# A first load of two rows a partition in place of one, and one load instead of two ahead of the entry barrier

## The chip, the cores and the metric

The kernel runs on one core of one Trainium2 chip. The metric is the device time of one execution in microseconds. The time before is 161.78 us, the median of 9 runs that lie between 161.64 and 162.16 us. Five kinds of engine matter here: VectorE (DVE in the profile) and ScalarE (ACT) compute, GpSimd (POOL) does small finishing work, SyncE (SP) issues every load and store, and the DMA engines move the data.

## The reference

The input `x` has 32 x 512 rows of 1024 float32 numbers, 16,384 rows or 67.1 MB. The result is one number a row:

```
relu_x = np.maximum(x, 0)
return np.mean(relu_x, axis=-1).astype(np.float32)
```

So every byte of 67.1 MB has to be read once from device memory, and 64 KB are written.

## The kernel before

The 16,384 rows lie one after another in memory, 4 KB each. The first 128 of them form a block of their own: partition p gets row p, into the tile `row0`. The other 16,256 rows are split so that each of the 128 partitions owns 127 consecutive rows (`J`), so the rows of neighbouring partitions start 127 rows, or 508 KiB, apart.

A partition's 127 rows are loaded in order, by SP, through one DMA queue: seven big loads of 16 rows a partition (`NB` = 16, 8 MB each, numbered t = 0 to 6) into three buffers in turn (`BUFS` = 3), then pieces of 7, 4, 2 and 1 rows (`row_pieces`), and then the last row in column pieces of 512, 256 and 256 (`col_pieces`). Each load has a semaphore of its own in `loaded`. Before a buffer is used again, SP waits in `buf_free` (lines 111 to 115) until ACT and DVE have finished with its previous content.

ACT and DVE share the rows: rows with an even number go to ACT (`act_row`, line 13: one activation with Relu whose accumulator gives the sum), rows with an odd number to DVE (`dve_row`, line 18). Both wait for the load in `rows` (line 144). POOL scales the sums by 1/1024 in `finish` (line 153). At the end the last full row is split between ACT and DVE, and of the very last row ACT takes 512 columns, DVE 256 and then, on line 197, the remaining 256 with the scaling and the sum of the row in one instruction. SP then stores `res` (line 205), clears the semaphores and waits on line 210 until the stores have landed.

The block `row0` is treated apart. ACT reduces it in one activation (line 164; its activation table is loaded just ahead, after the wait for the load), DVE turns the 128 results from a column into rows (line 168), and SP stores them with a small DMA (line 125) that is issued behind the load t = 3.

The program opens with entry barriers, in which every engine drains, reports and waits for a release (line 232 of the launch code and line 55 in the profile). The function `issue_ahead_of_entry_barrier(nc, n)` takes the first n loads out of SP's body and puts them ahead of SP's first drain, so that they are issued before the barrier. Before, n is 2: the load of `row0` (512 KB) and the load t = 0 (8 MB) go out ahead of the barrier, and t = 1 and t = 2 follow after it.

Of the kernel before, what the change touches and what calls it, by code (L numbers as in the profile page):

```python
# [9 lines left out]
ACT = mybir.ActivationFunctionType  # L10
# [15 lines left out]
def issue_ahead_of_entry_barrier(nc, n):  # L26


    entry = nc.cur_f.blocks[0].instructions
    for _ in range(n):  # L30
        body, load = next(
            (block.instructions, k)
            for block in nc.cur_f.blocks[1:]
            for k, ins in enumerate(block.instructions)
            if ins.opcode == "DMACopy"
        )
        first = body[load]
        assert first.engine == mybir.EngineType.SP and not first.sync_info.on_wait
        assert all(i.opcode in ("Drain", "EventSemaphore") or i.engine != first.engine for i in body[:load])
        del body[load]  # L40
        at = next(k for k, i in enumerate(entry) if i.engine == first.engine and i.opcode == "Drain")
        entry.insert(at, first)
# [3 lines left out]
def kernel(  # L46
# [10 lines left out]
    nc = tc.nc  # L57
    P = nc.NUM_PARTITIONS
    xf = x.flatten_outer_dims()
    R, D = xf.shape  # L60
    assert R % P == 0
    J = R // P
    inv = 1.0 / D

    xfirst, xmain = xf[:P, :], xf[P:, :]
    outfirst, outmain = out.flatten()[:P], out.flatten()[P:]
    J = J - 1
    xr = xmain.rearrange("(p j) d -> p j d", p=P, j=J)
    outr = outmain.rearrange("(p j) -> p j", p=P, j=J)

    NB = 16
    BUFS = 3
    full = J // NB

    row_pieces = [7, 4, 2, 1]
    assert full * NB + sum(row_pieces) + 1 == J
    col_pieces = [512, 256, 256]
    assert sum(col_pieces) == D

    def sbuf(name, *shape):  # L80
        return ctx.enter_context(nc.sbuf_tensor(name, list(shape), F32))

    bufs = [sbuf(f"rows{b}", P, NB, D) for b in range(BUFS)]
    sums, res, part = sbuf("sums", P, J), sbuf("res", P, J), sbuf("part", P, 2)


    last = sbuf("last", P, D + 2)
    scale = sbuf("scale", P, D // 4 + 2)

    row0, mean0, turned0 = sbuf("row0", P, D), sbuf("mean0", P, 32), sbuf("turned0", P, 32)  # L90


    loaded = [nc.alloc_semaphore(f"loaded{i}") for i in range(full + len(row_pieces) + len(col_pieces) + 1)]
# [1 line left out]
    first = nc.alloc_semaphore("first")  # L95
    stored = nc.alloc_semaphore("stored")
# [11 lines left out]
    def load(i, dst, src):  # L108
        nc.sync.dma_start(out=dst, in_=src).then_inc(loaded[i], 16)

    def buf_free(t):

        if t >= BUFS:
            nc.sync.wait_ge(act, t - BUFS + 1)
            nc.sync.wait_ge(dve, t - BUFS + 1)

    for t in range(full):
        buf_free(t)
        if t == 0:
            load(-1, row0[:, :], xfirst)  # L120
        load(t, bufs[t % BUFS][:, :, :], xr[:, t * NB:(t + 1) * NB, :])
        if t == BUFS:

            nc.sync.wait_ge(first, 2)
            nc.sync.dma_start(
                out=outfirst.rearrange("(q i) -> q i", i=32), in_=turned0[0:P:32, :],
            ).then_inc(stored, 16)
    j0 = full * NB
    buf_free(full)
    xt = bufs[full % BUFS]  # L130
    lo, i = 0, full
    for n in row_pieces:
        load(i, xt[:, lo:lo + n, :], xr[:, j0 + lo:j0 + lo + n, :])
        lo, i = lo + n, i + 1
    c = 0
    for w in col_pieces:
        load(i, last[:, c:c + w], xr[:, J - 1, c:c + w])
        c, i = c + w, i + 1
# [14 lines left out]
    def finish(after, lo, hi):  # L153
# [7 lines left out]
    nc.scalar.wait_ge(pool, 1)  # L161
    nc.vector.wait_ge(pool, 1)
    nc.scalar.wait_ge(loaded[-1], 16)
    nc.scalar.activation(  # L164
        out=row0[:, :], in_=row0[:, :], func=ACT.Relu, scale=inv, accum_out=mean0[:, 0:1],
    ).then_inc(first, 1)
    nc.vector.wait_ge(first, 1)
    nc.vector.transpose(turned0[:, :], mean0[:, :]).then_inc(first, 1)  # L168
    for t in range(full):
# [2 lines left out]
    lo, i = 0, full  # L172
    for n in row_pieces[:-1]:
        rows(i, xt, lo, n, j0)
        lo, i = lo + n, i + 1
# [12 lines left out]
        out=res[:, J - 2:J - 1], in0=part[:, 0:1], scalar1=part[:, 1:2], scalar2=inv, op0=ALU.add, op1=ALU.mult,  # L188
# [9 lines left out]
        out=last[:, 768:], in0=last[:, 768:], scalar=0.0, in1=scale[:, :], op0=ALU.max, op1=ALU.mult,  # L198
        accum_out=res[:, J - 1:J],
# [7 lines left out]
    used = [s.num for s in (*loaded, act, dve, pool, first)]  # L207
    assert used == list(range(used[0], used[0] + len(used)))
    nc.sync.sem_clear(range(used[0], used[-1] + 1))
    nc.sync.wait_ge(stored, 32).then_inc(stored, -32)  # L210

    for e, hint in zip(hinted, hints):
        e.br_lt(flag, 1, on_true="rows_begin", on_false="rows_end").branch_hint(hint)
    nc.br("rows_end", engines=[e for e in mybir.ALL_ENGINES if e not in (h.engine for h in hinted)])
    nc.switch_bb("rows_end")

    issue_ahead_of_entry_barrier(nc, 2)


# [28 lines left out]
```

## Time and profile before

| what | value |
|---|---|
| median of 9 runs | 161.78 us (161.64 to 162.16) |
| the profiled execution's own time | 161.89 us |
| its span | 160.5 us |
| DVE busy | 73.3 us, 46% of the span |
| ACT busy | 70.4 us, 44% of the span |
| DMA queue of the loads, share of the span | 97.3%, 67.18 MB |
| SP issues `row0`, t = 0, t = 1, t = 2 at | 0.00, 0.45, 1.92, 2.30 us |
| ACT has `row0` at | 3.44 us |
| ACT and DVE start on t = 0, 1, 2, ..., 6 at | 23.30, 42.66, 62.01, ..., 139.41 us |
| DVE's last instruction starts | 158.44 us |
| SP issues the last store at | 158.59 us |

Times inside an execution are counted from the start of the span, which is SP's first DMA issue. SPq is the queue of SP's issues. A DMA engine's packet is one descriptor: 4 KB for a row of `row0`, 64 KB for the 16 rows of a partition in a big load; a 4-byte packet is an engine's report to the semaphore. A load has landed when all 16 engines have reported.

### The profile page before, as it was taken

The page shows a single profiled execution, that of the slowest core. Times are in us where ns is not written, and L with a number is a line of the kernel's source. Part 1 is how long each engine was busy: PE and PEld are TensorE (multiplying, and loading weights), DVE is VectorE, ACT ScalarE, POOL GpSimd, SP SyncE. Part 2 cuts the span into 40 slices and gives each one's busy share as a digit, 9 for nine tenths or more (in the row PEclk, how much of TensorE's full clock was granted, in tenths as well). Part 3 has the DMA queues.
Part 4 walks back from the last instruction along what each step waited for, and adds up shares of the span by engine and source line. Part 5 has one row for each costly group of instructions (what it writes and reads, how often), then busy time and mean ns, then how long its engine had stood idle before and what let it go on. Part 6 is the DMA issues. An engine that isn't in the chain of part 4 may idle for free. (4 is left out here: it accounts for less than half of the span.)

```text
span 160.5 us, 347 instructions
## 1 busy us (share of the span) xinstructions
DVE 73.3 (46%) x131; ACT 70.4 (44%) x133; POOL 1.3 (1%) x9
## 2 busy tenths in 40 slices
DVE  0000019900399005970079500993009920299884
ACT  1400019900397005950079300991009900299983
POOL 1000000000000000000000000000000000000001
DMA  9969979979979989999899899899699699799991
GB/s 392 490 294 523 474 310 523 474 310 523 441 343 523 425 359 523 392 392 523 376 408 523 359 425 523 359 425 523 278 506 523 261 523 506 302 407 438 408 397 39
DMA packets 2313, 67.18 MB, mean 418 GB/s; under 512 B 393, under 2 KB 649, under 8 KB 1033
## 3 DMA queue, kind: packets, MB, share of 16 engines
q1 hardware_dynamic: 2312, 67.18, 97.3%
q14 instruction: 1, 0.00, 0.0%
HBM read 67.11 MB, written 0.07 MB: 418 GB/s over the span
## 5 line engine op out<-in xcount | busy, mean ns | idle before, releaser
L20 DVE TENSOR_SCALAR_CACHE_REDUCE rows<-rows 128x1024 f32<-128x1024 f32 (+1 forms) x63 | 72.1, 1208 | 78.9 <-DMA rows<-in_x_dram 78.8
L15 ACT ACTIVATE rows<-rows 128x1024 f32<-128x1024 f32 x64 | 66.2, 1035 | 84.1 <-DMA rows<-in_x_dram 83.9
L15 ACT ACTIVATION_READ_ACCUMULATOR rows<-rows 128x1 f32 x64 | 11.9, 187 | 0.0
L20 DVE DVE_READ_ACCUMULATOR rows<-rows 128x1 f32 x63 | 5.2, 83 | 0.0
L168 DVE STREAM_TRANSPOSE turned<-mean 128x32 f32<-128x32 f32 x1 | 0.2, 213 | 6.0 <-ACT row L164 6.0
L164 ACT ACT_TABLE_LOAD x1 | 1.3, 1283 | 3.4 <-DMA row<-in_x_dram 3.4
L157 POOL TENSOR_SCALAR res<-sums 128x112 f32<-128x112 f32 (+1 forms) x2 | 0.5, 248 | 154.1 <-DVE rows L20 154.1
L164 ACT ACTIVATE row<-row 128x1024 f32<-128x1024 f32 x1 | 1.1, 1056 | 0.0
L15 ACT ACTIVATE last<-last 128x512 f32<-128x512 f32 x1 | 0.6, 630 | 0.0
L20 DVE TENSOR_SCALAR_CACHE_REDUCE last<-last 128x256 f32<-128x256 f32 x1 | 0.4, 419 | 0.2 <-DMA last<-in_x_dram 0.2
L197 DVE SCALAR_TENSOR_TENSOR last<-last,scale 128x258 f32<-128x258 f32 x1 | 0.4, 428 | 0.1
L142 POOL MEMSET scale<- 128x258 f32 x1 | 0.3, 313 | 0.0
L187 POOL TENSOR_SCALAR res<-part 128x1 f32<-128x1 f32 x1 | 0.3, 264 | 0.6 <-DVE rows L20 0.6
L164 ACT ACTIVATION_READ_ACCUMULATOR row<-row 128x1 f32 x1 | 0.2, 187 | 0.0
L15 ACT ACTIVATION_READ_ACCUMULATOR last<-last 128x1 f32 x1 | 0.2, 186 | 0.0
L141 POOL MEMSET mean<- 128x32 f32 x1 | 0.1, 124 | 1.5 <-POOLq L55 1.5
L232 POOL MEMSET const-bfloat16-1.0<- 128x1 bf16 x1 | 0.1, 101 | 0.0
L232 POOL MEMSET const-uint8-127<- 128x1 uint8 x1 | 0.1, 101 | 0.0
L232 POOL MEMSET const-float32-0.0<- 128x1 f32 x1 | 0.1, 98 | 0.2 <-issue 0.2
L232 POOL MEMSET const-float32-1.0<- 128x1 f32 x1 | 0.1, 98 | 0.0
L197 DVE DVE_READ_ACCUMULATOR last<-last,scale 128x1 f32 x1 | 0.1, 83 | 0.0
L20 DVE DVE_READ_ACCUMULATOR last<-last 128x1 f32 x1 | 0.1, 82 | 0.0
## 6 DMA issues: line engine op xcount, KB each, us to landing
rows<-in_x_dram SPq DMA_DIRECT2D x1, 3584.0 KB, 37.9
rows<-in_x_dram SPq DMA_DIRECT2D x1, 2048.0 KB, 42.4
rows<-in_x_dram SPq DMA_DIRECT2D x1, 1024.0 KB, 44.4
row<-in_x_dram SPq DMA_DIRECT2D x1, 512.0 KB, 3.4
rows<-in_x_dram SPq DMA_DIRECT2D x1, 512.0 KB, 45.2
last<-in_x_dram SPq DMA_DIRECT2D x1, 256.0 KB, 45.4
last<-in_x_dram SPq DMA_DIRECT2D x2, 128.0 KB, 45.2
rows<-in_x_dram SPq DMA_DIRECT2D x7, 48.7
```

Source lines behind the costliest of these rows:

```text
L15: return nc.scalar.activation(out=src, in_=src, func=ACT.Relu, accum_out=acc)
L20: return nc.vector.tensor_scalar(out=src, in0=src, scalar1=0.0, scalar2=init, op0=ALU.max, op1=ALU.add, accum_out=acc,)
L141: nc.gpsimd.memset(mean0[:, :], 0.0)
L142: nc.gpsimd.memset(scale[:, :], inv).then_inc(pool, 1)
L157: nc.gpsimd.tensor_scalar(out=res[:, lo:hi], in0=sums[:, lo:hi], scalar1=inv, scalar2=0.0, op0=ALU.mult, op1=ALU.add,)
L164: nc.scalar.activation(out=row0[:, :], in_=row0[:, :], func=ACT.Relu, scale=inv, accum_out=mean0[:, 0:1],).then_inc(first, 1)
L168: nc.vector.transpose(turned0[:, :], mean0[:, :]).then_inc(first, 1)
L187: nc.gpsimd.tensor_scalar(out=res[:, J - 2:J - 1], in0=part[:, 0:1], scalar1=part[:, 1:2], scalar2=inv, op0=ALU.add, op1=ALU.mult,).then_i ...
L197: nc.vector.scalar_tensor_tensor(out=last[:, 768:], in0=last[:, 768:], scalar=0.0, in1=scale[:, :], op0=ALU.max, op1=ALU.mult, accum_out=r ...
L232: nc = _bacc.Bacc("TRN2", target_bir_lowering=False, num_devices=1)
```

## The change

The first two blocks of 128 rows are now both kept apart. Partition p gets row p of each, so `row0` holds two rows a partition and is loaded by one DMA of 1 MB with 256 descriptors of 4 KB. The rest is 126 rows a partition, so neighbouring partitions now start 504 KiB apart. The piece of 7 rows becomes one of 6; the big loads and the other pieces keep their sizes. ACT reduces the two rows of `row0` in two activations and reports after the second, DVE still turns them in one instruction, and SP stores them with two small DMAs, so the last wait is for 48 instead of 32. Only the load of `row0` is issued ahead of the entry barrier; the load t = 0 comes after it, ahead of t = 1 and t = 2.

```diff
-    xfirst, xmain = xf[:P, :], xf[P:, :]
-    outfirst, outmain = out.flatten()[:P], out.flatten()[P:]
-    J = J - 1
+    xfirst, xmain = xf[:2 * P, :].rearrange("(c p) d -> p c d", c=2), xf[2 * P:, :]
+    outfirst, outmain = out.flatten()[:2 * P], out.flatten()[2 * P:]
+    J = J - 2
...
-    row_pieces = [7, 4, 2, 1]
+    row_pieces = [6, 4, 2, 1]
...
-    row0, mean0, turned0 = sbuf("row0", P, D), sbuf("mean0", P, 32), sbuf("turned0", P, 32)
+    row0, mean0, turned0 = sbuf("row0", P, 2, D), sbuf("mean0", P, 32), sbuf("turned0", P, 32)
...
-            load(-1, row0[:, :], xfirst)
+            load(-1, row0[:, :, :], xfirst)
...
-            nc.sync.dma_start(
-                out=outfirst.rearrange("(q i) -> q i", i=32), in_=turned0[0:P:32, :],
-            ).then_inc(stored, 16)
+            for c in range(2):
+                nc.sync.dma_start(
+                    out=outfirst[c * P:(c + 1) * P].rearrange("(q i) -> q i", i=32), in_=turned0[c:P:32, :],
+                ).then_inc(stored, 16)
...
-    nc.scalar.activation(
-        out=row0[:, :], in_=row0[:, :], func=ACT.Relu, scale=inv, accum_out=mean0[:, 0:1],
-    ).then_inc(first, 1)
+    for c in range(2):
+        done = nc.scalar.activation(
+            out=row0[:, c, :], in_=row0[:, c, :], func=ACT.Relu, scale=inv, accum_out=mean0[:, c:c + 1],
+        )
+    done.then_inc(first, 1)
...
-    nc.sync.wait_ge(stored, 32).then_inc(stored, -32)
+    nc.sync.wait_ge(stored, 48).then_inc(stored, -48)
...
-    issue_ahead_of_entry_barrier(nc, 2)
+    issue_ahead_of_entry_barrier(nc, 1)
```

## The prediction

> **What bounds the kernel now.** I read the page's busy shares first, then the waits, then the timeline of the start and of the end, and last the records of single DMA packets and semaphore updates in the trace.
>
> ```profile
> span 160.5 us, 347 instructions
> ...
> DVE 73.3 (46%) x131; ACT 70.4 (44%) x133; POOL 1.3 (1%) x9
> ...
> q1 hardware_dynamic: 2312, 67.18, 97.3%
> ```
>
> Neither compute engine is busy half of the span; the queue of loads fills 97.3% of all 16 DMA engines' time. The waits say the same: ACT and DVE wait for nothing but loads.
>
> ```profile
> ACT rows L15 <- DMA rows<-in_x_dram: 83.9, 9, 17.4
> DVE rows L20 <- DMA rows<-in_x_dram: 78.8, 8, 17.1
> ```
>
> So the end is: when the stream of loads starts to flow, plus its bytes at the engines' rate, plus a tail behind the last piece. The timeline shows the start and the rate. Its columns are start, duration, engine, line, operation.
>
> ```profile
> 0.00 0.39 SPq L109 DMA_DIRECT2D row<-in_x_dram  x1
> ...
> 0.45 1.80 SPq L109 DMA_DIRECT2D rows<-in_x_dram  x2
> 1.93 0.12 POOL L141 MEMSET mean<- 128x32 f32 x1 [1.49 <-POOLq L55]
> ...
> 3.44 1.28 ACT L164 ACT_TABLE_LOAD   x1 [3.44 <-DMA row<-in_x_dram]
> ...
> 23.30 1.06 ACT L15 ACTIVATE rows<-rows 128x1024 f32<-128x1024 f32 x1 [17.42 <-DMA rows<-in_x_dram]
> ...
> 42.66 1.06 ACT L15 ACTIVATE rows<-rows 128x1024 f32<-128x1024 f32 x1 [10.94 <-DMA rows<-in_x_dram]
> ```
>
> From one big load to the next is 19.36 us (42.66 - 23.30), and the later ones agree (62.01, 81.36, 100.71, 120.06, 139.41). In the packet records a 64 KB packet takes 2.420 us (median of 896); each engine has 8 a load, 8 x 2.420 = 19.36. The engines are never without a packet in the middle, so nothing there can be won or lost except through the packets' own duration.
>
> The start is different. The packets of `row0` begin at 1.02 us, take 0.159 us each and follow at 0.1555 us. The engines finish their 8 between 2.44 and 2.93 us. Fifteen of the 16 start their first 64 KB packet between 2.50 and 2.93 us, but one of the three that had finished by 2.45 starts it only at 3.58: it idles some 1.13 us. That lag is never made up, because every engine has the same bytes. The last of the 16 reports of t = 0 comes at 23.27, the one before at 22.87; for the last piece of all it is 157.86 and 157.50. So 0.36 us of the end hangs on one engine that started late.
>
> The end, in the timeline:
>
> ```profile
> 155.30 1.22 DVE L20 TENSOR_SCALAR_CACHE_REDUCE rows<-rows 128x1024 f32<-128x1024 f32 x1
> ...
> 156.59 0.58 ACT L15 ACTIVATE rows<-rows 128x448 f32<-128x448 f32 x1
> ...
> 157.26 0.63 ACT L15 ACTIVATE last<-last 128x512 f32<-128x512 f32 x1
> ...
> 157.79 0.19 ACT L15 ACTIVATION_READ_ACCUMULATOR last<-last 128x1 f32 x1
> ...
> 158.08 0.43 DVE L197 SCALAR_TENSOR_TENSOR last<-last,scale 128x258 f32<-128x258 f32 x1
> ...
> 158.59 0.35 SPq L205 DMA_DIRECT2D out_dram<-res  x1
> ```
>
> The reader is to see that each piece is taken up as it lands and that the tail simply follows the landings.
>
> **The change part by part.** The sum is made against the profiled execution, 161.89 us (span 160.54, and 1.35 around it). It lies 0.11 over the median of the runs.
>
> *The entry barrier.* The instructions of the barrier show who holds it:
>
> ```profile
> L232 POOLq EVENT_SEMAPHORE  x2: 17/17/17, 1.1 to 1.2; - x2
> ...
> L232 SPq DRAIN  x1: 125/125/125, 0.9 to 0.9; - x1
> ```
>
> POOL's collecting semaphore at 1.07 comes right behind SP's drain (0.92 to 1.05); the others had drained by 0.48. With one issue less ahead of it, SP drains 0.47 us earlier (0.92 - 0.45), and what SP issues first after the barrier moves from 1.92 to about 1.45. That is now t = 0. Its issue is thus 1.0 us later than before (0.45 to 1.45); t = 1 and t = 2 follow at about 1.83 and 2.21 and are needed only 20 and 39 us later. ACT, DVE and POOL leave the barrier earlier too, for nothing: ACT waits for `row0` anyway.
>
> *The cover of the later issue.* `row0` is now 16 packets of 4 KB an engine, 8 x 0.1555 = 1.24 us more, so the engines finish it between 3.69 and 4.17. How long after its issue t = 0 can flow is bounded by rows of the trace: the last store's first packet came 0.84 us after its issue (158.59, 159.44), `row0`'s first packets 1.02 to about 1.3, most engines had t = 0 within 2.05 (0.45 to 2.50), and the late engine 3.14 (0.45 to 3.58). So t = 0 is there at 2.3, 2.75, 3.5 or, on one engine, 4.6 us. I take the middle two, as cold issues from SP of the same kind: it waits in the queue before `row0` is done, and no engine idles. If the issue of 256 descriptors takes longer than 0.39, it costs nothing until it is 0.2 us longer by the third of these values; issues of 128 descriptors took 0.33 to 0.49 and one of 4 descriptors 0.64, so the count does not show in them.
>
> *The bytes.* They are the same. Eight packets of 4 KB an engine take the place of 32 KB in the 7-row piece: 1.244 us for 8 x (1.062 - 0.911) = 1.21 us, where 0.911 is interpolated between the 16 KB (0.611) and 28 KB (1.062) packets. Cost +0.03.
>
> *The late engine.* If it is gone, the end follows the next engine, 0.36 us earlier: -0.36. If an engine is again 1.13 late, it starts t = 0 at 4.83 instead of 3.58 with 1.21 us of work more behind it: +0.04.
>
> *The row distance.* 504 instead of 508 KiB between partitions. In the trace 64 KB packets take 2.418 at best and 2.42 nearly always, but the first of each engine took up to 2.70, and in the wave around 32 us all took 2.43. So their duration does depend on how the streams lie. Bounds: all at 2.418 (8 x 7 x 0.002 = -0.1 us) to all at 2.434 (+0.8 us). I take 0, as 15 of 16 packets in mid-stream sit at 2.42.
>
> The Trainium skill's page "DMA: Bandwidth & Descriptors", section "Latency and other measured facts", speaks against this part: it lists copies whose partitions lie large powers of two apart as slower, 207 against 214 GB/s at 512 KiB, and the change moves the distance from 4 to 8 KiB short of 512. The same entry says that 4 KiB off was enough for the full rate, and the rows here, 508 KiB apart, run at 2.42 us a packet. If 504 KiB lost what the page has for 512, an estimate by its figures is 3.4% of 155 us, 5 us more; by the packet rows it is nothing.
>
> *ACT, DVE and the small store at the start.* A second activation of 1.06 us with its 0.19 read, all at 5 to 9 us, when ACT has nothing until 23.3: cover of 14 us, cost 0. It would cost its 1.04 us if t = 0 had landed. The second store of `turned0` has four packets of 128 B, each some 0.015 us on its engine, the late one among them: +0.015. Its issue (0.64) stands in SP's queue at 33 us, ahead of the load that waits for its buffer until 51.9, so nothing waits for it.
>
> *The tail.* The 6-row piece leaves DVE less time. Count from the start on t = 6 (139.41 before). DVE's rows follow each other at 1.14 us. The 4-row piece comes at 13.40 - 1.21 = 12.19, but DVE has 11 rows by then, until 12.54: late by 0.35. The 2-row piece comes at 14.68, DVE is free at 14.82; the 1-row piece at 15.97, DVE is free at 15.96. So it has just caught up, cost 0, and behind it DVE still has the 0.22 us that it waits for its first column piece. ACT has 11 rows x 1.04 = 11.4, before 12.19. The last store writes 504 instead of 508 bytes a partition: 0.
>
> Sum: -0.36 + 0.03 + 0.015 = -0.32, so 161.57 on the profiled execution's 161.89. The median of the runs is 0.11 lower, which I read as a late engine that is mostly a little less late; without it the runs would come down to the same place. I predict 161.56, 0.14% under the median. No change is what a measurement of this kernel cannot tell from zero, 0.2% or 0.32 us, so this lies within it.
>
> **The rivals.** *The late engine is late again.* What speaks for it: I can't say from the trace why it idled; its `row0` was done and the load had been issued 2 us before. If its cause is the change-over from one load to the next, it is in the new kernel too. Against: the 9 runs spread over 0.5 us, so it varies. With a gap of 1.13 us: 161.89 + 0.04 = 161.93, no change.
>
> *Slower: a later t = 0, or streams that hinder each other longer, at the first change-over.* Place: between `row0`'s last packet and an engine's first 64 KB. It decides from the point where any engine starts t = 0 after 5.0 us (4.79 is even with 161.89, and 162.10 is 0.2% over the median). The late engine's 3.14 us after the new issue would give 4.59, so it needs 0.4 more, an issue of `row0` of 0.8 us for its 256 descriptors; or a gap of 1.3 instead of 1.13. With twice the gap, 2.26, the start is at 5.96 and the time 161.89 + 1.17 = 163.06. For it: all first packets were slowed (2.42 to 2.70), so the streams do hinder each other at this point, and the row distance changes how. Against: 15 of 16 engines did not idle.
>
> *Slower all along.* Every packet at 2.434: 161.56 + 0.8 = 162.4 or more. Only a few waves show that now.
>
> *Faster by more.* The first packets' excess (0.02 to 0.28 over 2.42, in the mean 0.13) shrinks, since the engines finish 1 MB more spread out: 161.56 - 0.2 = 161.35.
>
> **How the numbers follow.** Back to back 0.45 (161.3 to 161.75, some two fifths of it under 161.46), the late engine as before 0.25 (a fifth of it over 162.10), slower at the change-over 0.20, slower all along 0.05, faster by more 0.05. Faster: 0.18 + 0.05, and a little for a gap that shrinks without going, 0.25. Slower: 0.20 + 0.05 + 0.05 = 0.30. Same: the rest, 0.45. Range 161.25 to 162.3: it leaves out the all-along case, half of the change-over case and a small part below, 0.2 in all.
>
> **What would show it.** SP's drain at about 0.45 and t = 0 issued at 1.4 to 1.8. ACT has `row0` at 4.6 to 4.8. With no late engine ACT and DVE start on t = 0 at 24.1 to 24.2 (23.30 + 1.21 - 0.33), and 24.5 with it; every later load 19.36 on. DVE without a pause from t = 6 to the last full row. It would be wrong if the steps between the big loads leave 19.36, if `row0` lands after 5 us, or if DVE reaches the split row after ACT.

## The result, and the profile after

The changed kernel takes 162.52 us, the median of 11 runs (162.31 to 163.12); the kernel before, 161.85 us over 34 runs. The ratio is 1.0043, with a 95% interval of 1.0032 to 1.0053: slower by 0.43%, some 0.7 us. The profiled execution took 162.43 us.

The page of the changed kernel has the same picture in the large, half-idle compute engines and a full queue of loads. The start, in its timeline:

```profile
0.00 0.45 SPq L109 DMA_DIRECT2D row<-in_x_dram  x1
...
1.50 1.39 SPq L109 DMA_DIRECT2D rows<-in_x_dram  x3
...
5.48 1.28 ACT L166 ACT_TABLE_LOAD   x1 [5.48 <-DMA row<-in_x_dram]
...
25.21 1.06 ACT L15 ACTIVATE rows<-rows 128x1024 f32<-128x1024 f32 x1 [16.25 <-DMA rows<-in_x_dram]
...
44.56 1.06 ACT L15 ACTIVATE rows<-rows 128x1024 f32<-128x1024 f32 x1 [10.92 <-DMA rows<-in_x_dram]
```

The reader is to see three things. SP issues t = 0 at 1.50 us, as foreseen. `row0` reaches ACT at 5.48, not at 4.6 to 4.8. And t = 0 is taken up at 25.21, not at 24.1 to 24.2. From there the step is 19.35 us again (44.56 - 25.21). So all of the loss has arisen by the time t = 0 has landed.

The end, in the same timeline, shows DVE without a pause, and at the split row (157.30) together with ACT, as foreseen:

```profile
153.86 1.21 DVE L20 TENSOR_SCALAR_CACHE_REDUCE rows<-rows 128x1024 f32<-128x1024 f32 x1
...
155.00 1.21 DVE L20 TENSOR_SCALAR_CACHE_REDUCE rows<-rows 128x1024 f32<-128x1024 f32 x1
...
156.01 1.06 ACT L15 ACTIVATE rows<-rows 128x1024 f32<-128x1024 f32 x1 [0.30 <-DMA rows<-in_x_dram]
156.14 1.21 DVE L20 TENSOR_SCALAR_CACHE_REDUCE rows<-rows 128x1024 f32<-128x1024 f32 x1
...
157.30 0.75 DVE L20 TENSOR_SCALAR_CACHE_REDUCE rows<-rows 128x576 f32<-128x576 f32 x1
157.30 0.58 ACT L15 ACTIVATE rows<-rows 128x448 f32<-128x448 f32 x1
...
159.34 0.35 SPq L208 DMA_DIRECT2D out_dram<-res  x1
```

The sum in the profiled executions: the last report of the last piece moves from 157.86 to 158.61, +0.75; from there to the last store's issue it is 0.73 in both; the last store takes 1.74 instead of 1.95 us, -0.21. Together +0.54, which is 162.43 - 161.89. (The last store's time is not the change's: with 504 bytes a partition it took 1.80 and 2.11 in the profiles of two kernels below.)

The records of single packets say where the 0.75 us arose:

| | before | after |
|---|---|---|
| the engines finish `row0` between | 2.44 and 2.93 us | 4.25 and 5.05 us (predicted: 3.69 and 4.17) |
| time that `row0`'s packets took over 0.159 each, mean of an engine | 0.23 us | 0.75 us |
| idle between `row0` and the first 64 KB packet | 1.13 us on one engine | none over 0.04 us |
| first 64 KB packets | 2.42 to 2.70 us | 2.42 to 2.72, one 3.68 us |
| last two of the 16 reports of the last piece | 157.50, 157.86 | 158.20, 158.61 |

Fifteen engines are late because `row0` itself went slowly: its packets between 1.1 and 2.9 us took up to 0.83 us instead of 0.16. That moves the last report but one by 0.70 (157.50 to 158.20). The sixteenth had 1.26 us in the first packet of t = 0, where before one engine had idled 1.13; its lag at the end is 0.41 instead of 0.36. Together that is the 0.75. The first 64 KB packets as a whole are no slower than before: 0.12 us over 2.42 in the mean of the 16, against 0.13. No engine was out of packets, so the cover held in the sense of the prediction, and yet it cost.

### The profile page after: what moved, and what is told of

Same layout as the page of the kernel before. It is cut to its first block, busy times and chain, and to the rows that moved or that the text cites. A ratio compares the mean times of both kernels' runs of the same rounds, so it can differ in the third digit from the quotient of the medians.

```text
span 161.1 us, 348 instructions
## 1 busy us (share of the span) xinstructions
DVE 73.0 (45%) x131; ACT 70.3 (44%) x133; POOL 1.3 (1%) x9
## 5 line engine op out<-in xcount | busy, mean ns | idle before, releaser
L15 ACT ACTIVATE rows<-rows 128x1024 f32<-128x1024 f32 (+1 forms) x63 | 65.1, 1035 | 82.9 <-DMA rows<-in_x_dram 82.8
L166 ACT ACTIVATE row<-row 128x1024 f32<-128x1024 f32 x2 | 2.1, 1048 | 0.0
```

What stands on the lines that cost most here:

```text
L15: return nc.scalar.activation(out=src, in_=src, func=ACT.Relu, accum_out=acc)
L166: done = nc.scalar.activation(out=row0[:, c, :], in_=row0[:, c, :], func=ACT.Relu, scale=inv, accum_out=mean0[:, c:c + 1],)
```

## The experiments

All ratios are against the kernel before, run on the same chip beside the variant, with 95% intervals. "Stretch" is what the first 64 KB packet of each engine took over 2.42 us, as the mean of the 16, in the one profiled execution; it leaves out idle time and `row0`'s own packets, which the table at the end has beside it. Diffs are against the changed kernel unless said otherwise.

**Both loads ahead of the barrier again.**

```diff
-    issue_ahead_of_entry_barrier(nc, 1)
+    issue_ahead_of_entry_barrier(nc, 2)
```

> The changed kernel with both loads ahead of the entry barrier again: only the order of issues is undone. Theory 'pattern' (the two rows of one partition, 512 KiB apart in memory, slow the first packets of the first load: 0.55 to 0.83 us instead of 0.17 to 0.39): row0 still reaches ACT at 5.4 to 5.5 us and the time stays at 162.5, within 0.15. Theory 'issue' (the later issue of t = 0 slows the start): row0 reaches ACT at about 4.6 and the time falls to 161.9. Theory 'count' (256 descriptors of one DMA come too slowly): as 'pattern', 162.5.

Ratio 0.9993 (0.9983 to 1.0004). The whole loss is gone, with two blocks, 126 rows and the two-row load in place. Its timeline:

```profile
0.00 0.45 SPq L109 DMA_DIRECT2D row<-in_x_dram  x1
...
0.49 2.32 SPq L109 DMA_DIRECT2D rows<-in_x_dram  x3
...
4.94 1.28 ACT L166 ACT_TABLE_LOAD   x1 [4.94 <-DMA row<-in_x_dram]
...
24.20 1.06 ACT L15 ACTIVATE rows<-rows 128x1024 f32<-128x1024 f32 x1 [15.77 <-DMA rows<-in_x_dram]
```

`row0` is there at 4.94 instead of 5.48, and t = 0 is taken up 1.01 us earlier than in the changed kernel. Every first 64 KB packet takes 2.42, stretch 0.00, and no engine is late (last two reports 157.71 and 157.72). So 'issue' holds for the time; the first packets of `row0` are still slow (eight took 0.7 to 0.9 us), so that part is not the later issue's.

**The first load in other forms, t = 0 still after the barrier.** Adjacent rows, rows 516 KiB apart, and two loads of one block each:

```diff
-    xfirst, xmain = xf[:2 * P, :].rearrange("(c p) d -> p c d", c=2), xf[2 * P:, :]
+    xfirst, xmain = xf[:2 * P, :].rearrange("(p c) d -> p c d", c=2), xf[2 * P:, :]
```

> The changed kernel with rows 2p and 2p+1 in partition p, so that its 8 KB lie together; the results of the first 256 rows come out in another order. 'Pattern': row0 reaches ACT at 4.6 to 4.7 us, 161.85. 'Issue': 5.4, 162.5. 'Count': 4.6, since it is 128 descriptors again if the two rows become one, 161.85.

Ratio 1.0077 (1.0058 to 1.0096), stretch 0.52, and one engine idle for at least 0.8 us: slower still.

```diff
-    xfirst, xmain = xf[:2 * P, :].rearrange("(c p) d -> p c d", c=2), xf[2 * P:, :]
+    xfirst, xmain = xf[:2 * (P + 1), :].rearrange("(c p) d -> p c d", c=2)[:P], xf[2 * P:, :]
```

> The changed kernel with row p and row 129 + p in partition p, so that the two rows are 516 instead of 512 KiB apart; row 128 is left out and row 256 read twice. 256 descriptors of 4 KB as in the change. 'Pattern', if it is the distance of 512 KiB: row0 reaches ACT at 4.6 to 4.7 us, 161.85. 'Issue' and 'count': 5.4, 162.5.

Ratio 1.0018 (1.0005 to 1.0032); the profiled execution, at 162.81 us the slowest of its 12, has a stretch of 0.39. In between the two theories, so it settles little: the loss is smaller than in the changed kernel, and not gone.

```diff
...
-            load(-1, row0[:, :, :], xfirst)
+            for c in range(2):
+                nc.sync.dma_start(out=row0[:, c, :], in_=xfirst[:, c, :]).then_inc(loaded[-1 - c], 16)
...
-    issue_ahead_of_entry_barrier(nc, 1)
+    issue_ahead_of_entry_barrier(nc, 2)
```

> The changed kernel with the two blocks loaded by two DMAs of 128 descriptors each, both ahead of the barrier; t = 0 still after it. 'Pattern': the engines read one block after the other, row0 is complete at 4.6 to 4.7 us, 161.85. 'Issue': t = 0 is later still, 162.5 or more. 'Count': 161.85. In all of these one engine is again 1.1 to 1.3 us late into t = 0, if that is a fixed cost of the change-over from 4 KB to 64 KB packets, and its last report comes 0.4 us behind the others'.

Ratio 1.0029 (1.0016 to 1.0041), stretch 0.15, one engine 0.33 us behind the next at the end. `row0` was complete on the engines at 3.85 to 4.22, where the prediction had it: its packets went faster, and the median was slower all the same (the profiled execution, 161.84, is near the fast end of its 12, 161.69 to 162.75). 'Pattern' and 'count' fall as the cause of the whole.

**One row, only its load ahead of the barrier** (against the kernel before: `issue_ahead_of_entry_barrier(nc, 1)`).

> The kernel before with only the load of row0 ahead of the entry barrier; one row, 127 rows a partition. Theory 'late issue' (an issue of t = 0 at about 1.5 instead of 0.45 us costs by itself, whatever covers it): slower by 0.5 to 0.9 us, 162.2 to 162.6 on a before of 161.7, with row0's packets or the first 64 KB packets stretched by several tenths. Theory 'cover' (it costs only as far as row0's packets don't cover it, and one row covers less than two): the engines idle from 2.5 to 2.9 until 2.8 to 3.5 us, so it is slower too, by 0.3 to 0.6, but with gaps instead of stretched packets.

Ratio 1.0076 (1.0052 to 1.0100). Both gaps and stretch: the engines finish `row0` at 2.49 to 2.95, start t = 0 at 2.63 to 3.98, and the first packets take 2.66 to 3.16 us, stretch 0.47. So the later issue costs some 1.2 us with a cover of one row and some 0.8 with two (1.0043 against 0.9993). In these two pairs more cover helps a little, but two rows are not enough; with two adjacent rows a partition the same step costs 1.3 us (1.0077, and 0.9994 in the last pair below).

**Two loads and t = 0, all three ahead of the barrier** (the two-load kernel above with n = 3).

> Two blocks by two DMAs, and t = 0, all three ahead of the barrier; 126 rows a partition. 'Late issue': 161.6, as fast as with the two-row load and t = 0 ahead (0.9993 of before), and the first 64 KB packets at 2.42 to 2.5. If the two-row load itself was what made that one clean, the first 64 KB packets stay at 2.5 to 2.7 and the time at 161.8 or above.

Ratio 1.0044 (1.0027 to 1.0060), stretch 0.62, against the 161.6 us that 'late issue' had foreseen. Here t = 0 was issued ahead of the barrier, at 0.91 us, and the loss came back. It is not the barrier, then. Nor is it simply the time of the issue: with t = 0 at 1.93 us, 1.0 us later, the same two loads were no slower (1.0029).

**t = 1 and t = 2 issued late**, in the changed kernel and in the kernel before:

```diff
         buf_free(t)
+        if t == 1:
+            nc.sync.wait_ge(first, 2)
```

> The changed kernel with t = 1 and t = 2 issued only when row0 has been reduced, at about 9 us instead of 1.9 and 2.4 us; t = 1 is needed at 24 us, so the wait itself costs nothing. Theory 'later issues' (the issues of t = 1 and t = 2 fall into the start of the stream and slow it): the stretched packets at 2.0 to 2.9 and of the first 64 KB wave go, 161.7 to 162.0. Theory 'late issue': they stay, 162.3 to 162.6.

Ratio 1.0037 (1.0021 to 1.0052), stretch 0.54.

> The kernel before with t = 1 and t = 2 issued only when row0 has been reduced, at about 6.3 us. 'Later issues': the first 64 KB packets fall from 2.43 to 2.70 to 2.42 and no engine is late, 161.3 to 161.5, faster than before. 'Late issue': no change, 161.7.

Ratio 0.9996 (0.9979 to 1.0013), stretch 0.19. The loss stays in the first and does not turn into a gain in the second, so the later issues have no part in it that these runs can tell.

**A first load with the row distance of t = 0**, once with t = 0 after the barrier and once, in the kernel before, ahead of it:

```diff
-            load(-1, row0[:, :, :], xfirst)
+            load(-1, row0[:, :, :], xr[:, 0:2, :])
```

> The changed kernel with a first load that reads the first two rows of each partition's own 126 (they are read again with t = 0; the results of the first 256 rows are wrong by that). Order of issues, bytes and descriptors (8 KB a partition) are those of e2_adjacent; only the distance between partitions in the first load, 504 KiB instead of 8 KiB, is now that of t = 0. Theory 'change of pattern' (the 16 streams get in each other's way when the distance between partitions changes, and then run free): the first 64 KB packets fall to 2.42 to 2.5, all stretch lies in row0, 161.6 to 162.0. Theory 'late issue': as e2_adjacent, first 64 KB packets of 2.6 to 3.4, 162.6 to 162.9.

Ratio 1.0063 (1.0044 to 1.0082), stretch 0.51, with a gap of at least 1.5 us on one engine. 'Change of pattern' falls here.

> The kernel before with a first load that reads the first row of each partition's own 127 (the results of the first 128 rows are wrong by that); both loads ahead of the barrier as before. 'Change of pattern': first 64 KB packets at 2.42 instead of 2.43 to 2.70, no engine late, 161.4. 'Late issue': no change, 161.7.

Ratio 1.0026 (1.0015 to 1.0037): slower than before, against both theories. Fifteen of the first 64 KB packets do take 2.42, but `row0`'s packets are stretched by 0.72 us an engine instead of 0.23. So this first load, with 508 KiB between its partitions, started slowly in its own packets; it is one profile.

**No small load ahead of t = 0**, first with `row0` loaded behind t = 0, then with no block apart at all (128 rows a partition, `row_pieces` = [8, 4, 2, 1]), both with n = 1.

> The kernel before with t = 0 as its first load, alone ahead of the barrier, and row0 behind it. Nothing that is issued after the barrier is needed before 20 us. 'Late issue': no late issue is left at the start, 161.4 to 161.6. 'Change of pattern': the cold start of 64 KB packets costs its stretch at 1 us, and the changes to row0 and back at 20 us cost theirs, 161.5 to 162.3.

Ratio 1.0028 (1.0017 to 1.0039). The first 64 KB packets take 2.65 to 3.99 us, although t = 0 is issued at 0.00 with nothing ahead of it and nothing needed behind it for 20 us.

> No block kept apart: 128 rows a partition, 512 KiB between partitions, t = 0 first and alone ahead of the barrier; last pieces of 8, 4, 2 and 1 rows. If the distance between partitions changes what a 64 KB packet takes in mid-stream, they are over 2.42 there and the time is 163 or more; if it matters only at the start, 161.4 to 161.8.

Ratio 0.9998 (0.9987 to 1.0008). The first packets are stretched here too (2.54 to 3.42 us, 0.56 in the mean); from the second on they take 2.42, at 512 KiB between partitions as at 508 and 504. So these three distances make no difference in mid-stream, and a load's first packets are slow even when nothing else goes on: from the issue of t = 0 to the end of its first packets it is 4.0 to 5.3 us in these two, where 1.0 of first delay and 2.42 would make 3.4.

**The lead.** If the first packets of a load go slowly for some 3 us after its issue, that time has to be covered by earlier packets; 2.8 us would then be too little. Four blocks in the first load make it longer:

```diff
-    xfirst, xmain = xf[:2 * P, :].rearrange("(c p) d -> p c d", c=2), xf[2 * P:, :]
+    xfirst, xmain = xf[:4 * P, :].rearrange("(c p) d -> p c d", c=4), xf[4 * P:, :]
...
-    row_pieces = [6, 4, 2, 1]
+    row_pieces = [4, 4, 2, 1]
...
+        if t == 2:
+            nc.sync.wait_ge(first, 2)
...
-            load(-1, row0[:, :, :], xfirst)
+            load(-1, row0[:, 0:4, :], xfirst)
...
```

Here `row0` is the third big buffer, so t = 2 waits until it has been reduced.

> The changed kernel with four blocks in the first load (2 MB, into the third big buffer, so t = 2 waits for their reduction), 124 rows a partition, last pieces 4, 4, 2, 1; only the first load ahead of the barrier. t = 0 is again issued at 1.5 us but not needed before 6.7. The shorter last pieces leave DVE behind by about 1.2 us at the end, here and in the next run alike. Theory 'lead' (t = 0 costs when it is issued too shortly before it is needed): first 64 KB packets at 2.42 to 2.5, the same time as the next run within 0.2 us. Theory 'late issue' (what counts is that t = 0 is issued when the stream is about to start or runs, and the cover doesn't matter): first 64 KB packets of 2.6 to 3.4, 0.5 to 1.0 us slower than the next run.

> The same with t = 0 ahead of the barrier too. Both theories: first 64 KB packets at 2.42, as with two rows and both loads ahead; about 162.7 with the slower end.

With t = 0 after the barrier 1.0077 (1.0064 to 1.0090), with t = 0 ahead of it 1.0073 (1.0060 to 1.0086): the same. Stretch 0.00 in both. Their timelines (the first with t = 0 after the barrier) have t = 0 taken up at the same time:

```profile
27.24 1.06 ACT L15 ACTIVATE rows<-rows 128x1024 f32<-128x1024 f32 x1 [13.74 <-DMA rows<-in_x_dram]
```

```profile
27.19 1.06 ACT L15 ACTIVATE rows<-rows 128x1024 f32<-128x1024 f32 x1 [13.74 <-DMA rows<-in_x_dram]
```

So with four rows ahead of it the later issue costs nothing: cover alone does it. (Both are slow by their end: with 13 rows to do after t = 6, DVE comes to the split row at 158.18, late by 1.3 us.)

Three blocks in the first load, done the same way (`c=3`, pieces of 5, 4, 2 and 1 rows), t = 0 after the barrier:

> The changed kernel with three blocks in the first load (1.5 MB, into the third big buffer), 125 rows a partition, last pieces 5, 4, 2, 1; only the first load ahead of the barrier. t = 0 is issued at 1.5 us and needed at about 5.5, a lead of 4.0 us, between the 2.8 of two rows and the 5.4 of four. By the counts of rows DVE's end costs nothing here (13 rows x 1.14 = 14.82 us after t = 6 lands, the split row lands at 14.76). Theory 'lead', with 3 to 4 us as what a load needs from its issue until it flows freely: first 64 KB packets at 2.42 or nearly, 161.5 to 161.9. If the lead has to be longer: 162.2 to 162.6.

Stretch 0.00 with a lead of 4.2 us, and the profiled execution took 161.88 us. But the ratio is 1.0024 (1.0008 to 1.0040) and the 12 runs lie between 161.81 and 162.79: the profiled execution is near the fastest, and what the slower ones lose is not seen in it.

**A tiny load between `row0` and t = 0**, all three ahead of the barrier.

```diff
...
+            load(-2, tiny[:, :], xfirst[:, 0, 0:8])
...
-    issue_ahead_of_entry_barrier(nc, 1)
+    issue_ahead_of_entry_barrier(nc, 3)
```

> The kernel with the two-row load and t = 0 ahead of the barrier (0.9993 of before), with a load of 4 KB in all (32 B a partition) issued between them, so that t = 0 goes out at about 0.95 instead of 0.49 us, still ahead of the barrier and 3.3 us before it is needed. 'Late issue', if 0.95 is too late already, as it seemed to be with two loads of one row ahead of t = 0: 162.1 to 162.6 and first 64 KB packets of 2.6 to 3.4. If only what comes after the barrier is late: 161.5 to 161.7, packets at 2.42.

Ratio 1.0024 (1.0011 to 1.0037). The profiled execution, at 161.59 the fastest of 12 up to 162.71, has a stretch of 0.01 with a lead of 3.4 us. The median is 0.3% above that of the two-row load without it (0.9993): the half microsecond by which t = 0 goes out later, or the tiny load itself, whose 128 packets of 32 B no run separates from it.

**Adjacent rows with t = 0 ahead of the barrier** (the slowest two-row form, n = 2).

> The first load of two adjacent rows a partition (with t = 0 after the barrier: 1.0077 of before) with t = 0 ahead of the barrier as well; the results of the first 256 rows come out in another order. Theory 'lead': t = 0 is issued at 0.45 and needed at 4.1, a lead of 3.6 us; its first packets fall from 2.6 to 3.4 to 2.42 or nearly, and the time to 161.5 to 161.8. If adjacent rows were slow for another reason: 162.3 or more.

Ratio 0.9994 (0.9981 to 1.0008), stretch 0.00, against 1.0077 and 0.52 with t = 0 after the barrier. The later issue alone made that variant slow.

**126 rows, the second block behind t = 0.**

```diff
...
-            load(-1, row0[:, :, :], xfirst)
+            load(-1, row0[:, 0, :], xfirst[:, 0, :])
...
+        if t == 0:
+            load(-2, row0[:, 1, :], xfirst[:, 1, :])
...
-    nc.scalar.wait_ge(loaded[-1], 16)
+        nc.scalar.wait_ge(loaded[-1 - c], 16)
...
-    issue_ahead_of_entry_barrier(nc, 1)
+    issue_ahead_of_entry_barrier(nc, 2)
```

> 126 rows a partition, but one block and t = 0 ahead of the barrier as in the kernel before; the second block is loaded between t = 0 and t = 1. The 126 rows alone: if they cost nothing, as before within 0.2 us, 161.6 to 161.9, and first 64 KB packets of 2.43 to 2.7 as in before. If the 504 KiB between partitions cost at the start, 162.1 or more.

Ratio 0.9979 (0.9967 to 0.9991): faster than the kernel before and, by the two ratios, 0.6% faster than the changed one; the best of all variants. Its timeline:

```profile
0.00 0.39 SPq L109 DMA_DIRECT2D row<-in_x_dram  x1
...
0.44 0.43 SPq L109 DMA_DIRECT2D rows<-in_x_dram  x1
1.93 0.33 SPq L109 DMA_DIRECT2D row<-in_x_dram  x1
...
2.30 0.92 SPq L109 DMA_DIRECT2D rows<-in_x_dram  x2
```

The 126 rows cost nothing. Why it gains 0.2% is not settled: in its profile no engine is late (last two reports 157.42 and 157.47), but that was so in the kernel before with t = 1 issued late, too (157.52, 157.57), and that one gained nothing.

All first loads that precede t = 0, ordered by the lead, from the issue of t = 0 to the first engine's end of `row0`. The three columns behind it are us an engine, as the mean of the 16, in the one profiled execution: what `row0`'s packets took over 0.159 each (0.309 for the 8 KB packets of two adjacent rows), the idle time between `row0` and t = 0, and the stretch.

| kernel | t = 0 issued at | lead | `row0`'s packets | idle | stretch | ratio |
|---|---|---|---|---|---|---|
| one row, n = 1 | 1.45 | 1.0 | 0.28 | 0.53 | 0.47 | 1.0076 |
| two loads, n = 2 | 1.93 | 1.9 | 0.32 | 0.00 | 0.15 | 1.0029 |
| before, t = 1 late | 0.44 | 2.0 | 0.22 | 0.00 | 0.19 | 0.9996 |
| before | 0.45 | 2.0 | 0.23 | 0.09, one gap of 1.13 | 0.13 | 1 |
| second block later | 0.44 | 2.2 | 0.22 | 0.00 | 0.09 | 0.9979 |
| before, rows of t = 0 | 0.45 | 2.6 | 0.72 | 0.00 | 0.03 | 1.0026 |
| adjacent rows, n = 1 | 1.45 | 2.6 | 0.35 | 0.18 | 0.52 | 1.0077 |
| rows of t = 0, n = 1 | 1.44 | 2.6 | 0.59 | 0.27 | 0.51 | 1.0063 |
| 516 KiB, n = 1 | 1.50 | 2.7 | 0.56 | 0.10 | 0.39 | 1.0018 |
| after, t = 1 late | 1.50 | 2.7 | 0.67 | 0.12 | 0.54 | 1.0037 |
| after | 1.50 | 2.8 | 0.75 | 0.02 | 0.12, one packet 1.26 | 1.0043 |
| two loads, n = 3 | 0.91 | 2.8 | 0.27 | 0.29 | 0.62 | 1.0044 |
| tiny load between, n = 3 | 0.99 | 3.4 | 0.37 | 0.00 | 0.01 | 1.0024 |
| adjacent rows, n = 2 | 0.44 | 3.6 | 0.52 | 0.00 | 0.00 | 0.9994 |
| two rows, n = 2 | 0.49 | 3.8 | 0.34 | 0.00 | 0.00 | 0.9993 |
| three rows, n = 1 | 1.50 | 4.2 | 0.68 | 0.00 | 0.00 | 1.0024 |
| four rows, n = 1 | 1.50 | 5.4 | 0.85 | 0.00 | 0.00 | 1.0077 (late end) |
| four rows, n = 2 | 0.49 | 6.2 | 0.57 | 0.00 | 0.00 | 1.0073 (late end) |

From 3.4 us on the first 64 KB packets are free or nearly so in all six profiles (none over 2.53 us); under 3 us they are stretched in all twelve (in one of them a single packet). Below 3 us the stretch does not follow the lead: with t = 0 at 0.45 and one row ahead it was mostly smaller, 0.03 to 0.19 at 2.0 to 2.6 us, than with t = 0 at 1.5 and two rows, 0.12 to 0.54 at 2.6 to 2.8.

And the stretch is not the loss. The three columns together are what an engine lost at the start. With t = 0 out by 0.5 us and one or two rows ahead they come to 0.31 to 0.52 in five kernels, and to 0.75 where the first load had the rows of t = 0; with t = 0 out later and one or two rows ahead, to 0.89 to 1.37 in seven. The other two of the later ones, two loads with n = 2 and the tiny load, come to 0.47 and 0.38 in profiled executions near the fast end of their runs, so their columns do not show what their medians lost. In the same way three rows and the tiny load, with leads of 4.2 and 3.4 us, have free first packets in a fast profiled execution and a median of 1.0024. The lead that is enough in the median is thus not known: it was 3.6 and 3.8 us with t = 0 out by 0.49, and 5.4 us with t = 0 at 1.50. What slows the packets, and what else decides how much, was not found. One profile a kernel is a small sample: the runs of a variant with a short lead spread over 0.4 to 1.3 us.

## Why the prediction was wrong

It gave 161.56 us, 161.25 to 162.3, no change as likeliest; measured were 162.52.

*The step that failed* is the cover of the later issue, which the sum had at nothing: t = 0 would be there at 2.75 or 3.5 us, `row0` would last until 3.69 at least, so no engine would idle and the issue 1.0 us later would be free. It cost 0.8 us. With that issue alone moved back, 1.0043 becomes 0.9993, and with adjacent rows 1.0077 becomes 0.9994, 1.3 us. The error under it was to ask only whether an engine has a packet: in the changed kernel none was without one for over 0.04 us, and the time went into the packets themselves. In the terms of the sum, what fifteen engines lose is +0.70 instead of +0.03 and +0.015, and the late engine is +0.05 instead of -0.36; that is the +0.75. With t = 0 ahead of the barrier again the late engine was gone, as the sum had it (last two reports 157.71 and 157.72).

Of its four values for how long after its issue t = 0 can flow, 0.84, 1.02 to 1.3, 2.05, and 3.14 us on the late engine, the prediction took the middle two and kept the last for one engine. All four say when a packet starts, and none when the stream flows: the first 64 KB packets were free on all engines only in profiles with leads of 3.4 us or more. The trace of before had a sign of this, first packets of 2.42 to 2.70 us and second ones of up to 2.73, which the prediction listed under the row distance and in a rival. That they belong to the short lead is argued from the table and not shown; and before, with a lead of 2.0 us, was as fast as two rows with 3.8.

*`row0` itself.* It was put at 16 x 0.1555 us an engine on top of the start of before. It took 0.6 to 0.9 us more, and landed at 5.48: "`row0` lands after 5 us" was one of the prediction's own signs of being wrong. With t = 0 ahead of the barrier the same load ended at 4.26 to 4.52 us, against 4.25 to 5.05, so part belongs to the two-row load (0.34 us an engine instead of 0.23) and part came with the later issue (0.75 in the changed kernel). How the issue of t = 0 at 1.5 us reaches back into `row0`'s packets of 1.1 to 2.9 us, some of which started ahead of it, is open. Nor is it so in every pair: with adjacent rows `row0` lost 0.35 us with the later issue and 0.52 without, and the four-row kernel with t = 0 ahead had 0.57.

*The late engine* was given 0.25 for coming again; it came, 1.26 us instead of 1.13, as a long packet and not as a gap. From the prediction's own formula, with an even start at 5.52 us (7.94 - 2.42) and 4.79 as the point of no change, the time is 161.89 + 0.73 = 162.62; the profile has 162.43, the last store being 0.21 shorter. This is near the prediction's rival of a later t = 0 at the first change-over, which had a chance of 0.20: its sign and its point of decision (5.0 us) held, its place only in part, since it looked between `row0`'s last packet and the first of t = 0, and the loss lay inside the packets on both sides. "15 of 16 engines did not idle", which was held against it, was no argument; in the changed kernel none idled, and it was slower.

*Right:* the barrier (SP's drain at 0.51 instead of 0.92, t = 0 issued at 1.50), the bytes, the row distance (taken as 0; 126 rows cost nothing, and 64 KB packets take 2.42 us at 504, 508 and 512 KiB), ACT's second activation and the second small store (0), and the tail: from the last report to the store's issue 0.73 us in both.

*Two readings of the trace of before* were not quite right, without weight in the sum. Not all first 64 KB packets were slowed: the late engine's own took 2.418 us, which is also the median of the 896 (the text has 2.420). And DVE did wait for something other than loads, 6.0 us for ACT's result of `row0`.

The rule on row distances that the prediction set against this was rightly not followed: the kernel with 128 rows a partition, 512 KiB apart, runs at 0.9998 of before. The Trainium skill's page "DMA: Bandwidth & Descriptors", section "Latency and other measured facts", has that rule for copies between tensors in device memory, where its 207 against 214 GB/s would be an estimated 3.4% at 512 KiB; these loads do not show it.

## What to carry to other kernels

In this kernel, which only streams, the end was fixed in the first few microseconds: the lag of the late engine when t = 0 lands (0.40 and 0.42 us, before and after) is still there in the last piece (0.36 and 0.41). In such a kernel do not take a later issue to be covered because every engine still has a packet. Here two rows, 2.8 us beyond the issue, did not cover it, four rows, 5.4 us, did, and an issue 1 us earlier was worth 0.5%. Before trusting a cover, compare the durations of the packets on both sides of the change-over with later ones, the first load's own packets too; and measure the medians, since one fast profiled execution can look clean.

## What the runs showed of the hardware

- A load's first 64 KB packets took 2.54 to 3.99 us when it was the first work of the queue (two kernels), and 2.42 in the median afterwards. With another load's packets ahead all 16 took 2.42 to 2.53 in the six profiles where the load had been issued 3.4 us or more before its need, and in none of the twelve with less.
- The distance between partitions, 504, 508 or 512 KiB, made no difference in mid-stream (2.42 us a packet). A first load of 4 KB packets 508 KiB apart lost 0.72 us an engine in its own packets, against 0.23 with the rows 4 KB apart (one profile each).
- With the same loads, t = 0 issued at 1.50 instead of 0.49 us moved the ratio from 0.9993 to 1.0043 with two rows ahead of it, and not at all with four (1.0077 and 1.0073, both with a late end).
- One issue fewer ahead of the entry barrier let SP drain at 0.51 instead of 0.92 us, and its next issue went out at 1.50 instead of 1.92.
